# Every third row of the first expert matrix, numbers 20 to 59, on GpSimd and ScalarE in place of VectorE

## The chip, the cores and the metric

One NeuronCore of a Trainium2 chip runs the whole program. The metric is the time of one execution on the device, in microseconds (us). Engines are named as in the profile: PE (TensorE), DVE (VectorE), ACT (ScalarE), POOL (GpSimd), SP (SyncE, which issues the plain transfers). POOL also issues the gathers, which are indirect DMAs.

## The reference

The model is two transformer blocks over 256 tokens of width 2048. The change lies in the second block, in its layer of 16384 small experts (`peer`). Each of eight heads scores two sets of 128 keys, takes the best 16 of each and the best 16 of their 256 sums, which gives each token 8 x 16 = 128 expert numbers. Then, for blocks of 128 tokens:

```python
def block(args):
    xb, ib, gb = args                      # tokens, expert numbers, gates
    act = jax.nn.gelu(jnp.einsum('tkd,td->tk', expert_u[ib], xb))
    return jnp.einsum('tk,tkd->td', act * gb, expert_v[ib])
```

The first einsum is the part at hand: for each token and each of its 128 experts, the row of `expert_u` (2048 values) is multiplied by the token and summed.

## The kernel before

Most of the kernel is a long run of projections, whose weights stream in through SP. Near 1500 us in it comes to the expert layer. There are 128 tokens on the 128 partitions, so a "row" n here is one gather: for slot s = n % 128 of token block tt = n // 128, every partition fetches the row of `expert_u` that its own token asks for, 128 x 2048 values, 1 MB. There are 256 such rows, 128 for each block of tokens.

`u_rows` (L1675) is a Python generator that writes this work out. `more` (L1679) asks for gathers (`gather`, L1661, issued by POOL at L1663) while a seat is free: ten seats for the first 128 rows, four after that (`seat`, L1676; two seats share one of the five tiles `rows`). Row n + 10 takes the seat of row n. A gather also needs the expert numbers of its head: 16 slots a head. At L1703 one DVE instruction multiplies the row by the tokens (`accT`, in PSUM, called `yt` in the profile) and sums over the 2048 columns, into one column of `wv` (`sm` in the profile).

The generators of several lanes are stepped in turn, each to its next `yield`, and every engine executes its instructions in the order in which they were written out. Other lanes at this place: `topk` (L1588) finds the 16 best of each head, on DVE (L1574 to L1585, L1608 to L1613, L1619, L1620) with two small steps on POOL (L1601 and L1603, L1615); heads 5, 6 and 7 are the last. `project1` (L449) runs the query projection on PE beside it; per group j of 128 query columns ACT copies the result out of PSUM (L1546), PE makes the scores (L1555) and ACT copies those (L1557). Groups 2h and 2h + 1 belong to head h. There are three PSUM banks for projections and one for scores.

After row 127 the tokens of the second block are turned into `accT` (L1659), ACT makes the weights (L1668), and the rest of the layer follows from them: rows 128 to 255, the scatter of weights (`spots`), the second expert matrix (L1847 and L1903), then the last projections.

Of the kernel before, what the change touches and what calls it, by code (L numbers as in the profile page):

```python
# [6 lines left out]
F32 = mybir.dt.float32  # L7
# [4 lines left out]
AF = mybir.ActivationFunctionType  # L12
OP = mybir.AluOpType
# [6 lines left out]
CH = 1024  # L20
# [205 lines left out]
def program(tc, A, out, stage=99, dbg=None):  # L226
# [7 lines left out]
    hip = pool("hip", 3)  # L234
# [3 lines left out]
    def psum(name, bufs):  # L238

        p = contextlib.ExitStack()  # L240
        t = p.enter_context(tc.tile_pool(name=name, bufs=bufs, space=bass.MemoryType.PSUM))
        banks_.append(p)
        return t

    def psum_close(n):
        for _ in range(n):
            banks_.pop().close()
# [5 lines left out]
    V, S, G, PE, SP = nc.vector, nc.scalar, nc.gpsimd, nc.tensor, nc.sync  # L253
# [1264 lines left out]
    accT = rowp.tile([128, 2048], F32, name="yt", tag="yt")  # L1518
# [20 lines left out]
    wv = sm.rearrange("p a b -> p (a b)").rearrange("p (t s) -> p t s", t=2)  # L1539
# [116 lines left out]
    def turn(tt):  # L1656

        for j in range(16):
            PE.transpose(accT[:, j * 128:j * 128 + 128], xg[:, j, tt * 128:tt * 128 + 128], ident)  # L1659

    def gather(dst, src, n):  # L1661
        tt, s = divmod(n, 128)
        G.indirect_dma_start(dst, None, src, bass.IndirectOffsetOnAxis(ap=idx[:, tt, s:s + 1], axis=0))  # L1663

    def weights(tt):

        w = wv[:, tt]
        S.activation(w, w, AF.Gelu_apprx_tanh, scale=rtok[:, tt, 0:1])  # L1668
        G.tensor_mul(w, w, gate_[:, tt])
        p = pair("wt") if tt else bank(bgN, "pn")  # L1670
        PE.transpose(p[:, :128], w, ident)
        S.copy(wT[:, tt * 128:tt * 128 + 128], p[:, :128])
        flags[("w", tt)] = True

    def u_rows():  # L1675
        seat = [n % 10 if n < 128 else n % 4 for n in range(256)]  # L1676
        done, busy, ask = [0], {}, [0]

        def more(most):  # L1679

            while most and ask[0] < 256 and seat[ask[0]] not in busy and flags.get(("idx", ask[0] % 128 // 16)):
                m = ask[0]
                gather(row[seat[m]], A["w_u"], m)
                busy[seat[m]] = m
                ask[0] += 1
                most -= 1

        heads = lambda: sum(bool(flags.get(("idx", h))) for h in range(8))
        turn(0)
        while heads() < 2:  # L1690
            more(1)
            yield
        for n in range(256):
            tt, s = divmod(n, 128)
            for _ in range(2 if heads() < 8 else 0):
                more(1)
                yield
            more(2)
            while n >= ask[0]:
                yield  # L1700
                more(1)
            r = row[seat[n]]
            V.scalar_tensor_tensor(r, r, 1.0, accT, op0=OP.mult, op1=OP.mult, accum_out=wv[:, tt, s:s + 1])  # L1703
            del busy[seat[n]]
            if s == 127:
                if tt:
                    psum_close(2)
                    pairs_.update(sacc=psum("sacc", 1), tok=psum("tok", 1), wt=psum("gap", 2))
                    pairs_["sp"] = pairs_["wt"]
                else:  # L1710
                    turn(1)
                weights(tt)
            yield
        flags["u"] = True
# [144 lines left out]
    for n, lane in enumerate((2, 3, 5, 6)):  # L1859
        lanes.add(lane, topk(n, cU if n > 1 else cT))  # L1860
    lanes.add(0, slots_())
    lanes.add(4, u_rows())
    lanes.add(1, spots(0))
    lanes.add(1, spots(1))
# [100 lines left out]
```

## Time and profile before

| | |
|---|---|
| median of 3 runs | 2922.49 us (2918.72 to 2924.63) |
| the profiled execution's own time | 2921.0 us |
| its span | 2919.1 us |
| PE busy | 2292.5 us, 79% |
| DVE busy | 2002.7 us, 69% |
| ACT busy | 1185.9 us, 41% |
| POOL busy | 874.4 us, 30% |
| L1703 on DVE, 256 rows | 580.0 us |
| L1663 on POOL, 256 gathers of the first matrix | 241.6 us |

The span runs from the first to the last instruction of the profiled execution; 1.9 us of its own time lie around it. Shares of busy time are means over the whole kernel. The rows of the first matrix occupy DVE from 1554.5 to 2250.4 us. In the rows below, a bracket at the end of a timeline row tells how long the engine had been idle and what ended that.

### The profile page before, as it was taken

How to read it: one execution, taken by the hardware profiler on the slowest of the kernel's cores; microseconds unless marked ns; L12 is line 12 of the kernel's file. 1: busy time of each engine (PE TensorE's matmuls, PEld its weight loads, DVE VectorE, ACT ScalarE, POOL GpSimd, SP SyncE). 2: the span in 40 equal slices, each digit the busy share in tenths (PEclk: the TensorE clock that was granted, in tenths of full speed). 3: DMA queues.
4: the chain of work that ended last, by engine and by line, in shares of the span. 5: the costliest groups of instructions: out<-in, count | busy, mean ns of one | idle time of the engine just before them, and what ended most of it. 6: DMA issues, size and time to landing. Idle time of an engine off the chain costs nothing.

```text
span 2919.1 us, 39399 instructions
## 1 busy us (share of the span) xinstructions
PE 2292.5 (79%) x14635; PEld 2095.4 (72%) x14635; DVE 2002.7 (69%) x2641; ACT 1185.9 (41%) x2529; POOL 874.4 (30%) x1168
## 2 busy tenths in 40 slices
PE   8999999999999999999999100012211999999999
PEld 8887899888888999998998000012211988888789
DVE  5455566555556565666638999989898866666665
ACT  4355555444444454444431000058881355400043
POOL 3201215211111010223024344333333655555520
PEclk9999999999999999999999555555665699999999
DMA  6443455656655555553559889999998699999955
GB/s 224 148 130 123 125 161 179 195 188 188 194 186 192 186 174 190 171 169 109 162 186 379 347 310 422 421 400 420 401 420 346 234 397 409 409 407 409 409 200 167
DMA packets 174672, 765.09 MB, mean 262 GB/s; under 512 B 19584, under 2 KB 22048, under 8 KB 141200
## 3 DMA queue, kind: packets, MB, share of 16 engines
q1 hardware_dynamic: 99216, 353.83, 36.3%
q0 software_dynamic: 75264, 408.75, 35.0%
q8 instruction: 115, 1.88, 0.3%
q14 instruction: 77, 0.63, 0.1%
HBM read 757.77 MB, written 4.21 MB: 261 GB/s over the span
## 4 chain that ended last, share of the span: by engine, by line
PE 61%; DMA 11%; issue 10%; DVE 8%; POOL 8%; ACT 1%; POOLq 0%; SPq 0%; DVEq 0%; ACTq 0%
PE acc L411 11%; PE acc L1903 8%; PE acc L386 6%; PE acc L388 6%; PE acc L387 6%; POOL rows L1663 6%; PE acc L412 6%; DMA rows<-w_vs,idx 5%; DMA rows<-w_u,idx 4%; PE acc L485 3%; PE acc L483 3%; PE acc L484 3%; DVE rows L1703 3%; PE sp L1794 1%; DMA raw<-w_vd 1%
## 5 line engine op out<-in xcount | busy, mean ns | idle before, releaser
L350 DVE TENSOR_TENSOR wlo<-raw,whi 128x1024 fp32r<-128x1024 f32 (+1 forms) x501 | 615.2, 1236 | 390.9 <-ACT whi L349 384.0
L349 ACT CAST whi<-raw 128x1024 fp32r<-128x1024 f32 (+1 forms) x501 | 520.0, 1042 | 363.6 <-PE acc L387 131.8
L1703 DVE SCALAR_TENSOR_TENSOR rows<-rows,yt 128x2048 f32<-128x2048 f32 x256 | 580.0, 2284 | 40.8 <-DMA rows<-w_u,idx 36.6
L1903 PE MATMUL acc<-G,raw 128*128 128x256 f32 x2048 | 452.5, 382 | 11.9 <-DMA raw<-w_vd 10.9
L1903 PEld LDWEIGHTS acc<-G,raw 128*128 128x128 f32 x2048 | 388.1, 191 | 69.9 <-DMA raw<-w_vd 16.8
L1847 DVE SCALAR_TENSOR_TENSOR sacc<-rows,sm,sacc 128x1024 f32<-128x1024 f32 x254 | 327.3, 1289 | 143.4 <-DMA rows<-w_vs,idx 140.7
L1663 POOL DMA_INDIRECT rows<-w_u,idx x256 | 241.6, 944 | 392.5 <-DVE rows L1703 299.7
L1663 POOL DMA_INDIRECT rows<-w_vs,idx x256 | 247.5, 967 | 151.2 <-DVE sacc L1847 87.1
L411 PE MATMUL acc<-xl,whi 128*128 128x512 f32 x704 | 248.2, 391 | 0.0
L411 PE MATMUL acc<-xh,whi 128*128 128x512 f32 x704 | 248.1, 391 | 0.0
L1762 PE MATMUL sp<-P,Q 128*128 128x128 f32 x256 | 58.1, 419 | 213.9 <-ACT P L1758 213.9
L1762 PEld LDWEIGHTS sp<-P,Q 128*128 128x128 f32 x256 | 55.1, 327 | 217.1 <-ACT P L1758 217.1
L564 POOL TENSOR_TENSOR acc_sq<-acc_sq,sq 128x256 f32<-128x256 f32 x63 | 56.8, 902 | 500.4 <-ACT sq L563 498.8
L485 PE MATMUL acc<-ring,wlo 128*128 128x256 f32 x704 | 199.3, 283 | 0.1
L483 PE MATMUL acc<-ring,whi 128*128 128x256 f32 x704 | 199.3, 283 | 0.1
L484 PE MATMUL acc<-ring,whi 128*128 128x256 f32 x704 | 199.2, 283 | 0.0
L412 PE MATMUL acc<-xh,wlo 128*128 128x256 f32 x704 | 197.2, 280 | 0.6 <-DVE wlo L350 0.6
L412 PE MATMUL acc<-xl,wlo 128*128 128x256 f32 x704 | 197.1, 280 | 0.0
L1191 POOL TENSOR_TENSOR hT<-cF 128x256 f32<-128x256 f32 x44 | 71.8, 1632 | 372.9 <-ACT whi L349 342.9
L1659 PE MATMUL yt<-keep,xg 128*128 128x128 f32 x32 | 5.6, 350 | 201.9 <-DVE rows L1703 201.4
L386 PE MATMUL acc<-xh,whi 128*128 128x256 f32 x520 | 150.5, 289 | 3.1 <-ACT whi L349 1.8
L411 PEld LDWEIGHTS acc<-xh,whi 128*128 128x128 f32 x704 | 131.7, 187 | 28.9
(505 smaller groups left out, 5524.0 us busy)
## 6 DMA issues: line engine op xcount, KB each, us to landing
raw<-w_gu SPq DMA_DIRECT2D x176, 512.0 KB, 3.9
raw<-w_vd SPq DMA_DIRECT2D x128, 512.0 KB, 6.8
raw<-w_down SPq DMA_DIRECT2D x88, 512.0 KB, 4.4
raw<-w_out SPq DMA_DIRECT2D x32, 512.0 KB, 3.5
raw<-w_pq SPq DMA_DIRECT2D x32, 512.0 KB, 7.1
raw<-w_pg SPq DMA_DIRECT2D x32, 512.0 KB, 3.8
raw<-w_b SPq DMA_DIRECT2D x24, 512.0 KB, 3.6
raw<-w_lat SPq DMA_DIRECT2D x18, 512.0 KB, 3.7
```

The lines of the kernel that those rows point to most:

```text
L349: S.copy(hi[j][:, a:b], raw[j][:, a:b])
L350: V.tensor_sub(lo[j][:, a:b], raw[j][:, a:b], hi[j][:, a:b].bitcast(F32))
L386: PE.matmul(ps, wh, xh, start=start, stop=False, **k)
L411: PE.matmul(ps, wh, xh.both(k), start=k == 0, stop=False, skip_group_check=True)
L412: PE.matmul(ps[:, :T], wl, xh[:, k], start=False, stop=k == kb - 1, skip_group_check=True)
L483: PE.matmul(o, wh, ah, start=(k == 0 and j % 2 == 0), stop=False, skip_group_check=True)
L484: PE.matmul(o, wh, al, start=False, stop=False, skip_group_check=True)
L485: PE.matmul(o, wl, ah, start=False, stop=(k == nk - 1), skip_group_check=True)
L1663: G.indirect_dma_start(dst, None, src, bass.IndirectOffsetOnAxis(ap=idx[:, tt, s:s + 1], axis=0))
L1703: V.scalar_tensor_tensor(r, r, 1.0, accT, op0=OP.mult, op1=OP.mult, accum_out=wv[:, tt, s:s + 1])
L1847: V.scalar_tensor_tensor(sacc, r, w, sacc, op0=OP.mult, op1=OP.add)
L1903: PE.matmul(o, w, gs_[k // 16][:, k % 16], start=(k == 0 and j % 2 == 0), stop=k == 127, skip_group_check=True)
```

## The change

Of the rows 18 to 59 every third one (n % 3 == 2: rows 20, 23, ... 59, fourteen of them) is no longer done by L1703. POOL multiplies it in two halves of 1024 columns by a copy of the tokens in SBUF, in place, and ACT sums the product with an Identity activation. ACT makes the copy of the tokens once, at row 12, in two tiles of the pool `hip`. The seat of such a row is given free one row later (`late`), so that the gather which takes it stands behind the next row. In the changed kernel the lines from 1703 on have other numbers: the copies are L1710, the product L1714, the sum L1715, and the DVE instruction that was L1703 is L1718.

```diff
@@ u_rows @@
         turn(0)
+        late, yt = [], []
...
             r = row[seat[n]]
-            V.scalar_tensor_tensor(r, r, 1.0, accT, op0=OP.mult, op1=OP.mult, accum_out=wv[:, tt, s:s + 1])
-            del busy[seat[n]]
+            while late:
+                del busy[late.pop()]
+            if n == 12:
+
+                for k in range(2):
+                    yt.append(hip.tile([128, CH], F32, name="yt2", tag="whi"))
+                    S.copy(yt[k], accT[:, k * CH:k * CH + CH])
+            if 18 <= n < 60 and n % 3 == 2:
+                for k in range(2):
+                    b = r[:, k * CH:k * CH + CH]
+                    G.tensor_mul(b, b, yt[k])
+                S.activation(r, r, AF.Identity, accum_out=wv[:, tt, s:s + 1])
+                late.append(seat[n])
+            else:
+                V.scalar_tensor_tensor(r, r, 1.0, accT, op0=OP.mult, op1=OP.mult, accum_out=wv[:, tt, s:s + 1])
+                del busy[seat[n]]
```

What stands in a row on POOL, around row 20, before: the first L1663 is the gather of row 29, the two after it those of rows 30 and 31, then come the small steps of head 5's top 16. The bracket names the engines and queues whose counts an instruction waits for (DMASW are the gathers' own queues).

```order
L1663 DMA rows_15111<-w_u,idx 128x2048 [waits DMASW0_49,DVE_49]
L1663 DMA rows_15107<-w_u,idx 128x2048 [waits DMASW1_49,DVE_49]
L1663 DMA rows_15107<-w_u,idx 128x2048 [waits DMASW2_49,DVE_49]
L1601 TENSOR_TENSOR cT<-cT 128x256 x2
L1603 CAST cT<-cT 128x64 [waits DVE_49]
L1663 DMA rows_15108<-w_u,idx 128x2048 [waits DMASW3_49,DVE_49]
```

And the same place on POOL now, from behind the gather of row 29 to that of row 33:

```order
L1714 TENSOR_TENSOR rows_15107<-rows_15107,yt_15623 128x1024 [waits Activation_49]
L1714 TENSOR_TENSOR rows_15107<-rows_15107,yt_15625 128x1024 [waits Activation_49]
L1663 DMA rows_15107<-w_u,idx 128x2048 [waits DMASW1_49,Activation_49]
L1601 TENSOR_TENSOR cT<-cT 128x256 [waits DVE_49] x2
L1603 CAST cT<-cT 128x64 [waits DVE_49]
L1663 DMA rows_15107<-w_u,idx 128x2048 [waits DMASW2_49]
L1663 DMA rows_15108<-w_u,idx 128x2048 [waits DMASW3_49,DVE_49]
L1714 TENSOR_TENSOR rows_15108<-rows_15108,yt_15623 128x1024
L1714 TENSOR_TENSOR rows_15108<-rows_15108,yt_15625 128x1024
L1615 TENSOR_TENSOR cT<-cT 128x256 [waits DVE_49,Pool_49]
L1615 TENSOR_TENSOR cT<-cT 128x256 x3
L1663 DMA rows_15108<-w_u,idx 128x2048 [waits DMASW4_49,Activation_49]
```

The two products of row 20 stand behind the gather of row 29, and the gather of row 30, which is to fill row 20's seat, stands right behind the products and waits for ACT, that is for row 20's sum. The same holds for the other thirteen rows and the gathers ten rows later; behind the products of rows 23, 29 and 35 the four L1615 of heads 5, 6 and 7 come first.

On ACT, before, around the copy of query group 11 out of PSUM (the first L1546 here) and the scores of groups 11 and 12:

```order
L1546 COPY cK<-acc 128x256 [waits PE_49,Activation_49]
L1557 ACTIVATE sc<-pa,rtok 128x128 [waits PE_49]
L1557 ACTIVATE sc<-pa,rtok 128x128
L1546 COPY cK<-acc 128x256 [waits PE_49,Activation_49]
L1557 ACTIVATE sc<-pa,rtok 128x128 [waits PE_49]
```

And now:

```order
L1546 COPY cK<-acc 128x256 [waits PE_49,Activation_49]
L1715 ACTIVATE rows_15107,sm<-rows_15107 128x2048 [waits DMASW7_49,Pool_49]
L1557 ACTIVATE sc<-pa,rtok 128x128 [waits PE_49]
L1557 ACTIVATE sc<-pa,rtok 128x128
L1546 COPY cK<-acc 128x256 [waits PE_49,Activation_49]
L1715 ACTIVATE rows_15108,sm<-rows_15108 128x2048 [waits DMASW1_49,DMASW2_49,DMASW0_49,Pool_49]
L1557 ACTIVATE sc<-pa,rtok 128x128 [waits PE_49]
```

The sums of rows 20, 23, 26, 29 and 32 stand ahead of the score copies of groups 11, 12, 13, 14 and 15. On DVE nothing else moves: fourteen instructions are gone from its row.

## Rows read from the trace of the kernel before

**Rows 1.** The chain that ended last, by line, shares of the span.

```profile
PE acc L411 11%; PE acc L1903 8%; PE acc L386 6%; PE acc L388 6%; PE acc L387 6%; POOL rows L1663 6%; PE acc L412 6%; DMA rows<-w_vs,idx 5%; DMA rows<-w_u,idx 4%; PE acc L485 3%; PE acc L483 3%; PE acc L484 3%; DVE rows L1703 3%; PE sp L1794 1%; DMA raw<-w_vd 1%
```

**Rows 2.** Busy time of each engine in three stretches; clock, DMA share, GB/s.

```profile
1650.00:1700.00 50.00, 0.00 (x0) 0.00 (x0) 48.26 (x129) 0.00 (x0) 19.42 (x27) 0.50 0.68 251
1700.00:1750.00 50.00, 1.42 (x4) 0.73 (x4) 49.08 (x60) 2.57 (x6) 23.09 (x31) 0.50 0.86 335
1750.00:1800.00 50.00, 0.00 (x0) 0.00 (x0) 50.00 (x45) 0.00 (x0) 21.58 (x23) 0.50 1.01 422
```

**Rows 3.** Timeline of POOL: start, duration, line, [idle before, releaser].

```profile
1636.05 0.94 POOL L1663 DMA_INDIRECT rows<-w_u,idx  x1 [1.26 <-DVE rows L1703]
...
1670.17 1.19 POOL L1601 TENSOR_TENSOR cU<-cU 128x256 f32<-128x256 f32 x2 [2.13 <-DVE cU L1582]
1671.58 0.24 POOL L1603 CAST cU<-cU 128x64 f32<-128x64 uint32 x1 [0.22 <-DVE cU L1585]
...
1681.54 2.78 POOL L1615 TENSOR_TENSOR cU<-cU 128x256 f32<-128x256 f32 x4 [2.18 <-DVE cU L1613]
...
1734.42 0.94 POOL L1663 DMA_INDIRECT rows<-w_u,idx  x1 [1.26 <-DVE rows L1703]
1736.63 0.94 POOL L1663 DMA_INDIRECT rows<-w_u,idx  x1 [1.26 <-DVE rows L1703]
...
1813.40 0.94 POOL L1663 DMA_INDIRECT rows<-w_u,idx  x1 [0.30 <-issue]
```

**Rows 4.** L1703 counted from its start to 1846.2 and to 1922 us.

```profile
L1703 DVE SCALAR_TENSOR_TENSOR rows<-rows,yt x97: 2227/2281/2289, 1554.5 to 1843.8; 128x2048 f32<-128x2048 f32 x97
L1703 DVE SCALAR_TENSOR_TENSOR rows<-rows,yt x128: 2227/2282/2289, 1554.5 to 1921.3; 128x2048 f32<-128x2048 f32 x128
```

**Rows 5.** Timeline of DVE, rows 97 and 127.

```profile
1846.24 2.29 DVE L1703 SCALAR_TENSOR_TENSOR rows<-rows,yt 128x2048 f32<-128x2048 f32 x1 [0.19 <-DMA rows<-w_u,idx]
...
1921.34 2.29 DVE L1703 SCALAR_TENSOR_TENSOR rows<-rows,yt 128x2048 f32<-128x2048 f32 x1 [0.19 <-DMA rows<-w_u,idx]
```

**Rows 6.** L1663: its gathers up to 1636.5 us; landing of those of 1650 to 1720.

```profile
L1663 POOL DMA_INDIRECT rows<-w_u,idx x30: 939/945/1068, 1540.5 to 1636.1; - x30
DMA to landing us min/median/max: 5.3/5.6/8.5
```

**Rows 7.** Products on POOL by shape: count, busy us, mean ns.

```profile
L1191 POOL TENSOR_TENSOR hT<-cF 128x256 f32<-128x256 f32 x44 | 71.8, 1632 | 372.9 <-ACT whi L349 342.9 <-DVE cF L1190 29.9
L1789 POOL TENSOR_TENSOR P<-P,acc_sq 128x512 f32<-128x512 f32 x16 | 17.3, 1084 | 15.8 <-DVE P L1781 14.8 <-ACT acc_sq L1672 0.9
L733 POOL TENSOR_TENSOR cL<-cL 128x512 f32<-128x512 f32 x2 | 2.6, 1294 | 23.4 <-ACT cL L732 23.4
L1037 POOL TENSOR_TENSOR cC<-cC,cM 128x1024 f32<-128x1024 f32 x1 | 2.8, 2825 | 3.0 <-DMA cC<-sguw 3.0
```

**Rows 8.** ACT by shape: a pass over 1024 columns; reading out a sum.

```profile
L349 ACT CAST whi<-raw 128x1024 fp32r<-128x1024 f32 x493 | 514.0, 1047 | 359.8 <-PE acc L387 128.0 <-PE acc L484 126.4 <-PE acc L411 61.7
L928 ACT ACTIVATION_READ_ACCUMULATOR nsat<-nsat 128x1 f32 x32 | 6.0, 186 | 0.0
```

**Rows 9.** Timeline of ACT: query group 11 copied out, and its scores.

```profile
1584.07 0.37 ACT L1546 COPY cK<-acc 128x256 f32<-128x256 f32 x1 [2.88 <-PE acc L456]
1587.92 0.62 ACT L1557 ACTIVATE sc<-pa,rtok 128x128 f32<-128x128 f32 x2 [3.47 <-PE pa L1555]
```

**Rows 10.** Timeline of DVE: head 5's first steps, row 21, its next steps, row 22.

```profile
1637.91 0.87 DVE L1574 MAX8 cT<-sc 128x8 f32<-128x128 f32 x4
...
1641.55 2.27 DVE L1703 SCALAR_TENSOR_TENSOR rows<-rows,yt 128x2048 f32<-128x2048 f32 x1
1643.75 0.09 DVE L1703 DVE_READ_ACCUMULATOR rows<-rows,yt 128x1 f32 x1
...
1645.73 1.00 DVE L1574 MAX8 cT<-cT 128x8 f32<-128x256 f32 x2 [0.83 <-POOL cT L1601]
1646.64 2.27 DVE L1703 SCALAR_TENSOR_TENSOR rows<-rows,yt 128x2048 f32<-128x2048 f32 x1
```

## The prediction

> **What bounds the kernel now.** The chain of waits comes first [rows 1]: it passes through the gathers (POOL L1663, the DMA of the first matrix) and through L1703, so this stage is on the path to the end. The table of stretches comes next [rows 2]. From 1650 to 1750 us VectorE is busy 48 to 49 of 50 us and the DMA engines only 0.68 and 0.86 of theirs; from 1750 the DMA share is 1.01. So VectorE, which finds the top 16 and multiplies rows, is the limit up to about 1750, and the DMA engines after it. The timelines say the same. After the top 16, gathers leave POOL every 2.21 us and each has waited 1.26 us for L1703 to free a seat [rows 3]. From row 97 to row 127, which the counts identify [rows 4], VectorE has waited for the DMA at both ends, and 30 rows take 1921.34 - 1846.24 = 75.1 us, 2.50 us a row [rows 5]. What the first half costs is therefore read at one place: the time at which row 127 starts, 1921.34. All later work (weights, scatter, second matrix) hangs on that row and moves with it.
>
> **What the change removes.** Fourteen instructions of VectorE. At the spacing of 2.21 us [rows 3] that is 30.9 us of VectorE's time. It can bring at most what the DMA engines have idle: 0.32 x 50 + 0.14 x 50 = 23 us [rows 2].
>
> **What it adds on GpSimd.** This engine's queue is also the one that issues the gathers. I add up what stands in it from the gather of row 29 to the gather of row 69, which waits for the last sum, that of row 59. The gather of row 29 is the thirtieth and starts at 1636.05 [rows 3, 6].
> Gathers: 40 x (0.94 + 0.30 us of issue) [rows 3] = 49.6 us.
> Products: 28 of 128x1024. The trace has one such shape, 2.83 us, and 512 columns at 1.08 and 1.29 us [rows 7]; the top-16 products of 256 columns take 0.60 and 0.70 us each beside the row instructions [rows 3]. From 0.70 at 256 and 1.08 at 512 a line gives 1.86 at 1024; twice 1.08 is 2.17. I take 2.2, near the row of 1.08, and keep 1.86 and 2.83: 28 x 2.2 = 61.6 us (52 to 79).
> [...]
> Waits for sums: each of fourteen gathers stands behind a pair of products and waits until ScalarE has summed that row. A pass over 1024 columns takes 1.047 us there and reading the sum out 0.19 [rows 8]; two passes less one start-up, with the read-out, come to about 2.15, and two handovers add some 0.35: 2.5 us. In three of the fourteen places the four L1615 of a head (2.78 us [rows 3]) stand between and cover it: 11 x 2.5 = 27.5 us (bounds 1.9 and 3 us each: 21 to 33).
> Top-16 steps of heads 5, 6 and 7: 1.19 + 0.24 + 2.78 = 4.2 us each [rows 3], 12.6 us.
>
> **What it adds by ScalarE's order.** The scores of group 11, copied at 1587.92 now [rows 9], stand behind the sum of row 20, whose row is multiplied only after the gather of row 29. So they wait from about 1588 to 1644: product from 1637.0 to 1641.4, sum to 1643.6, copies to 1644.3. PE has one bank for scores, stops at those of group 12 and loses its clock (the clock is 0.50 where PE idles [rows 2]); that is hidden, because groups 13 to 15 are gated by the sums of rows 26, 29 and 32 anyway, some 10 us apart. But VectorE needs groups 10 and 11 for head 5. Its first steps take 1641.55 - 1637.91 = 3.64 us [rows 10], so they end at 1648.0 and not at 1641.55. GpSimd, done with the gather of row 30 at 1645.1, waits 2.9 us for them; then for the next steps, which stand behind row 21 (2.2 + 1.15 us, to 1651.4), 2.0 us; then for row 22 (0.9 + 2.2 us) some 1.5 us more, with the durations of [rows 10]. That is 6.4 us at head 5; heads 6 and 7 meet the same order behind rows 26 and 32: 3 x 6.4 = 19.2 us (10 to 30).
> The two copies of the tokens (2 x 1.05 us [rows 8]) fall into ScalarE's idle time, 2.9 us and more before each step there [rows 9]: nothing.
>
> **The sum.** 49.6 + 61.6 + 27.5 + 12.6 + 19.2 = 170.5 us: the gather of row 69 starts at 1806.6. By then the gathers issued before it have landed, so it lands after 5.6 us, the median where the DMA engines had idle time [rows 6], at 1812.2. From there the DMA engines are the limit as before: 58 rows x 2.50 = 145 us, and row 127 starts at 1957.2 against 1921.34, 36 us later. VectorE's 30.9 us are inside this: it waits for rows in place of multiplying them. The profiled execution took 2921.0 us, 1.9 of them outside the span, and 2921 + 36 = 2957; the median of the runs shown is 1.5 us above it. I predict 2958.
> In other words, once the top 16 is over three rows cost GpSimd 3 x 1.24 + 2 x 2.2 + 2.5 = 10.6 us, 3.5 a row, where VectorE alone took 2.21 and the DMA engines need 2.50.
>
> **The rivals.**
> First, faster: GpSimd hides its part. It is idle more than half of every stretch now (19.4 to 23.1 of 50 us busy [rows 2]), which speaks for it. If a product takes 1.9 us and the next gathers don't have to wait for the sum, three rows cost 3.72 + 3.8 = 7.5 us, just the DMA's 3 x 2.50; then VectorE's gift fills the idle DMA time and 23 us go: 2898. Against it stands the changed order: the gather behind each pair waits for ScalarE. With that wait the product would have to take 0.64 us, less than what 256 columns take.
> Second, no change: the products run at 0.7 us, so that the 170.5 us shrink by 28 x 1.5 = 42 to 128; the gather of row 69 then starts at 1764 and lands at 1770, and it need not land before 1921.34 - 145 = 1776 for row 127 to come when it does now: 2921 to 2926. Only a product of 1024 columns that costs as much as one of 256 would do it.
> Third, far slower: GpSimd and VectorE disturb each other. L1191 takes 1.63 us for 256 columns, beside conversions on VectorE, where the top-16 products take 0.60 to 0.70 [rows 3, 7]. At four times 1.63 a product costs 6.5 us, 28 x 4.3 = 120 us more: 3078. The undisturbed figures come from this very stage, with L1703 running beside them, which speaks against it. The Trainium skill (GPSIMD Engine Reference, section 1) has GpSimd share its SBUF interface with VectorE, with contention where VectorE's instruction reads two SBUF inputs or runs in a two-port mode; L1703 reads one input from PSUM, so by this rule too the time would stay at the forecast, and the chance of this rival stays small.
> That the instructions don't move as told isn't a rival: the changed order shows it.
>
> **How the numbers follow.** The forecast, GpSimd's queue as the bound of rows 20 to 69, has 0.84. Its own range: products 52 to 79 in place of 61.6, waits 21 to 33, head delays 10 to 30, not all at one end together, give -16 to +25 around 2957, so 2941 to 2982. Faster gets 0.05, no change 0.02, far slower 0.05; 0.04 is left for a smaller loss of 6 to 20 us, if heads and sums hide more than I think. The range 2938 to 2984 holds about 0.85 of this. 0.2%, 6 us, is about what a measurement of this kernel can tell from no change: faster 0.05, same 0.03, slower 0.92.
>
> **What would show it.** Right: products (L1714) of about 2.2 us; GpSimd's gathers every third time idle for 2.5 us behind ACT's L1715; after the top 16 three gathers per 10.6 us; VectorE waiting for rows between 1740 and 1810, where it waits for none now; a DMA share well under 1 up to about 1810; the scores of group 11 near 1644; row 127 near 1957; later stages of unchanged length. Wrong: products under 1 us or gathers that don't wait for L1715 (then the first two rivals), products over 4 us (the third), or a stage after row 127 that shrinks.

## The result, and the profile after

| | before | after |
|---|---|---|
| median of the runs | 2923.37 us (4 runs, 2918.72 to 2924.63) | 2968.11 us (4 runs, 2964.86 to 2972.16) |
| ratio after / before, 95% interval | | 1.0143 [1.0122, 1.0163] |
| profiled execution / its span | 2921.0 / 2919.1 us | 2972.16 / 2970.4 us |
| start of row 0 (first row instruction on VectorE) | 1554.52 us | 1563.21 us |
| start of row 127 | 1921.34 us | 1972.03 us |
| row 0 to row 127 | 366.8 us | 408.8 us |
| row 127 to the end of the span | 997.8 us | 998.4 us |

The change makes the kernel slower: by 44.7 us between the medians (1.53%), by 1.43%, some 42 us, in the ratio. 2958 was forecast, and the forecast range holds the result. Of the 50.7 us by which row 127 starts later in the two profiles, 8.7 are there before row 0, ahead of all that the change touches: the 1408 matmuls of the projection at L411 took 399 ns each in this execution and 391 ns in the other, 9 us in all; why they did stays open. The stage between row 0 and row 127 is longer by 42.0 us, and all that follows has kept its length.

The stretches of the changed kernel, to be held against [rows 2] (columns: window, length, busy us of PE, PEld, DVE, ACT and POOL with their instructions, granted clock, DMA share, GB/s):

```profile
1650.00:1700.00 50.00, 26.30 (x92) 21.36 (x92) 38.46 (x117) 8.90 (x16) 30.71 (x27) 0.70 0.68 255
1700.00:1750.00 50.00, 2.14 (x7) 1.47 (x7) 40.30 (x80) 9.46 (x16) 34.00 (x35) 0.50 0.54 195
1750.00:1800.00 50.00, 0.50 (x2) 0.18 (x1) 24.06 (x23) 10.45 (x12) 35.81 (x24) 0.50 0.83 308
1800.00:1850.00 50.00, 0.00 (x0) 0.00 (x0) 38.38 (x34) 4.00 (x4) 31.14 (x27) 0.50 0.89 348
```

VectorE is no longer the limit: of 50 us it is busy 24 between 1750 and 1800, where it was busy 50. But the DMA engines have not taken over. Their share sinks to 0.54 between 1700 and 1750 (0.86 before) and stays below 1.01 up to 1850. Neither of the two engines of [rows 2] is full, so a third sets the pace, and it is not one with a high busy share either: POOL stands at 31 to 36 of 50.

POOL's timeline shows what it does. First the steady cycle after the top 16, to be held against [rows 3]; the columns are start, duration, engine, line, and in brackets the idle time before it with what ended it:

```profile
1761.60 4.67 POOL L1714 TENSOR_TENSOR rows<-rows,yt 128x1024 f32<-128x1024 f32 x2
1768.57 0.98 POOL L1663 DMA_INDIRECT rows<-w_u,idx  x1 [2.31 <-ACT rows L1715]
1769.86 0.95 POOL L1663 DMA_INDIRECT rows<-w_u,idx  x1 [0.30 <-DVE rows L1718]
1771.11 0.95 POOL L1663 DMA_INDIRECT rows<-w_u,idx  x1 [0.30 <-issue]
1772.08 2.35 POOL L1714 TENSOR_TENSOR rows<-rows,yt 128x1024 f32<-128x1024 f32 x1
```

From one pair of products to the next it takes 1772.08 - 1761.60 = 10.48 us, three gathers of which the first stands idle 2.31 us for ScalarE's sum: 3.5 us a row, where the DMA engines need 2.50. The forecast for this cycle was 10.6 us.

Then the place around row 20 in the same view, where the sum blocks the scores:

```profile
1646.82 0.94 POOL L1663 DMA_INDIRECT rows<-w_u,idx  x1 [1.26 <-DVE cT L1574]
1647.78 4.64 POOL L1714 TENSOR_TENSOR rows<-rows,yt 128x1024 f32<-128x1024 f32 x2
1654.73 0.98 POOL L1663 DMA_INDIRECT rows<-w_u,idx  x1 [2.31 <-ACT sc L1557]
1657.98 1.20 POOL L1601 TENSOR_TENSOR cT<-cT 128x256 f32<-128x256 f32 x2 [2.27 <-DVE cT L1582]
1661.60 0.24 POOL L1603 CAST cT<-cT 128x64 f32<-128x64 uint32 x1 [2.42 <-DVE cT L1585]
1661.99 0.98 POOL L1663 DMA_INDIRECT rows<-w_u,idx  x1
1664.65 0.95 POOL L1663 DMA_INDIRECT rows<-w_u,idx  x1 [1.69 <-DVE rows L1718]
```

and ScalarE's timeline of the same time:

```profile
1578.05 0.37 ACT L1546 COPY cK<-acc 128x256 f32<-128x256 f32 x1 [2.88 <-PE acc L456]
1614.38 1.93 ACT L1710 COPY yt<-yt 128x1024 f32<-128x1024 f32 x2 [35.96 <-DVE rows L1718]
...
1652.46 1.91 ACT L1715 ACTIVATE rows<-rows 128x2048 f32<-128x2048 f32 x1 [29.28 <-POOL rows L1714]
1654.27 0.19 ACT L1715 ACTIVATION_READ_ACCUMULATOR rows<-rows 128x1 f32 x1
1654.36 0.61 ACT L1557 ACTIVATE sc<-pa,rtok 128x128 f32<-128x128 f32 x2
```

The scores of group 11 (L1557, the last line) are copied from 1654.36 to 1654.97. On the clock of before (8.7 us less) that ends at 1646.3, where 1644.3 was forecast. A releaser has to be read with care here: POOL's gather at 1654.73 names "ACT sc L1557", but its seat is that of row 20, so it waited for the sum at 1652.46, whose release ScalarE gave about the time at which it began the scores. On VectorE's timeline, row 12 stops for the copies of the tokens, and later the first step of head 5 for these scores:

```profile
1616.34 2.29 DVE L1718 SCALAR_TENSOR_TENSOR rows<-rows,yt 128x2048 f32<-128x2048 f32 x1 [1.99 <-ACT yt L1710]
...
1654.74 0.68 DVE L1574 MAX8 cT<-sc 128x8 f32<-128x128 f32 x3 [7.98 <-ACT sc L1557]
```

The first line is one that the prediction did not have: the copies at row 12 (L1710, above) wait 35.96 us for VectorE to have read the tokens' tile in row 11, and VectorE's row 12 waits 1.99 us for the copies. Both engines only read that tile in PSUM, and yet in this trace they take turns at it. The second line has its like at heads 6 and 7; the three waits come to 21.8 us of VectorE's time (13.8 in the line below and the 7.98 above):

```profile
DVE cU L1574 <- ACT sc L1557: 13.8, 2, 8.0
```

The durations by shape, L1714 being the product, L1715 the sum and L1718 the row instruction on VectorE (min, median and max in ns, first and last start):

```profile
L1714 POOL TENSOR_TENSOR rows<-rows,yt x28: 2340/2356/2372, 1647.8 to 1816.2; 128x1024 f32<-128x1024 f32 x28
...
L1718 DVE SCALAR_TENSOR_TENSOR rows<-rows,yt x242: 2228/2287/2290, 1563.2 to 2299.4; 128x2048 f32<-128x2048 f32 x121
...
L1715 ACT ACTIVATE rows<-rows x14: 1909/1909/1911, 1652.5 to 1818.6; 128x2048 f32<-128x2048 f32 x14
L1715 ACT ACTIVATION_READ_ACCUMULATOR rows<-rows x14: 185/186/188, 1654.3 to 1820.4; 128x1 f32 x14
```

No sign is seen of one engine slowing the other: all 28 products lie within 32 ns, those of 1700 to 1750, where VectorE is busy 40 of 50 us, as well as those of 1750 to 1800, where it is busy 24, and VectorE's rows have kept 2.28 us [rows 4]. The rival with contention is out by this view alone, and so is the one with a cheap product.

### The profile page after: what moved, and what is told of

It is laid out like the page before. It is cut to its first block, busy times and chain, and to the rows that moved or that the text cites. A ratio compares the mean times of both kernels' runs of the same rounds, so it can differ in the third digit from the quotient of the medians.

```text
span 2970.4 us, 39454 instructions
## 1 busy us (share of the span) xinstructions
PE 2311.7 (78%) x14635; PEld 2100.0 (71%) x14635; DVE 1981.8 (67%) x2613; ACT 1215.9 (41%) x2559; POOL 941.5 (32%) x1196
## 4 chain that ended last, share of the span: by engine, by line
PE 60%; DMA 11%; issue 10%; POOL 9%; DVE 8%; ACT 1%; SPq 0%; POOLq 0%; ACTq 0%; DVEq 0%
PE acc L411 11%; PE acc L1918 8%; PE acc L386 6%; PE acc L388 6%; PE acc L387 6%; DMA rows<-w_u,idx 6%; PE acc L412 5%; POOL rows L1663 5%; DMA rows<-w_vs,idx 5%; PE acc L485 3%; PE acc L483 3%; PE acc L484 3%; DVE rows L1718 2%; PE sp L1809 1%; POOL rows L1714 1%
## 5 line engine op out<-in xcount | busy, mean ns | idle before, releaser
L1718 DVE SCALAR_TENSOR_TENSOR rows<-rows,yt 128x2048 f32<-128x2048 f32 x242 | 552.0, 2285 | 82.9 <-DMA rows<-w_u,idx 76.5
L1663 POOL DMA_INDIRECT rows<-w_u,idx x256 | 242.3, 947 | 369.9 <-DVE rows L1718 229.3
L1663 POOL DMA_INDIRECT rows<-w_vs,idx x256 | 248.2, 969 | 145.0 <-DVE sacc L1862 68.4
L411 PE MATMUL acc<-xl,whi 128*128 128x512 f32 x704 | 252.7, 399 | 0.0
L411 PE MATMUL acc<-xh,whi 128*128 128x512 f32 x704 | 252.7, 399 | 0.0
L411 PEld LDWEIGHTS acc<-xh,whi 128*128 128x128 f32 x704 | 132.3, 188 | 32.9
```

The source lines that it names most:

```text
L411: PE.matmul(ps, wh, xh.both(k), start=k == 0, stop=False, skip_group_check=True)
```

## The experiments

All are built on the changed kernel. Since the time before row 0 differs from run to run, each was read in two ways: by its ratio to the kernel before, and by the stage from row 0 to row 127 in its profile (366.8 us before, 408.8 after). A stage is read from one profiled execution; the only kernel of the experiments that was profiled twice gave 359.2 and 360.2 us, so a difference of 1 to 2 us says little.

**Seats given back one product later.** The gather behind a pair of products then takes the seat of the row before that.

```
-            while late:
-                del busy[late.pop()]
+            while len(late) > (n < 60):
+                del busy[late.pop(0)]
```

> The seat of a row that GpSimd multiplied is given back one such row later, so that the gather behind a pair of products takes a seat whose sum is long done; products, sums and ScalarE's order stay. Theory A (GpSimd's queue: products and waits for sums between its gathers): after the top 16 three rows cost 10.46 - 2.31 = 8.15 us, the waits <-ACT L1715 of POOL go (17.3 + 6.9 us, about 24), row 127 comes some 20 to 25 us earlier than with the change, +20 to +25 us against the kernel before. Theory B (what costs is ScalarE's order: the score copies that stand behind sums make the top 16 late): the scores stay blocked, so the loss stays, +40 to +45. Theory C (it is the products alone): +40 too, since the waits only move to another place.

Measured: 2956.02 us, ratio 1.0085 [1.0062, 1.0108], +25 us; row 0 to row 127 takes 391.5 us, 17.3 less than with the change. POOL's timeline no longer has the wait:

```profile
1746.87 4.66 POOL L1714 TENSOR_TENSOR rows<-rows,yt 128x1024 f32<-128x1024 f32 x2
1751.69 0.99 POOL L1663 DMA_INDIRECT rows<-w_u,idx  x1 [0.16 <-issue]
1752.98 0.94 POOL L1663 DMA_INDIRECT rows<-w_u,idx  x1 [0.30 <-issue]
1754.23 0.95 POOL L1663 DMA_INDIRECT rows<-w_u,idx  x1 [0.30 <-issue]
1755.20 4.64 POOL L1714 TENSOR_TENSOR rows<-rows,yt 128x1024 f32<-128x1024 f32 x2
```

Three rows take 8.33 us, and yet the scores of group 11 still come at 1652.48. So the gathers' waits for the sums are a cost of their own, of about 17 us; theories B and C, which left the loss at 40, are out as explanations of the whole. The rest, +25, is still there.

**Products without sums.**

```
-                S.activation(r, r, AF.Identity, accum_out=wv[:, tt, s:s + 1])
```

> The fourteen sums on ScalarE are left out (so these rows have no result); the products on GpSimd stay. This takes away both the gathers' waits for sums and what blocks the score copies. Theory A: of the 170.5 us reckoned in GpSimd's queue, the 27.5 of waits and the 19.2 of head delays go, the products' 65 stay: row 127 comes 35 to 45 us earlier than with the change, 0 to +10 us against the kernel before; three rows after the top 16 take 8.1 to 8.4 us. Theory C (the products alone bound it): +30 or more, as with the change. Theory D (VectorE's relief of 30.9 us is real once the waits are gone): -15 to -20, faster than before.

Measured: 2934.46 us, ratio 1.0017 [0.9995, 1.0038]; 374.6 us from row 0 to row 127, 16.9 less than with the seats alone held back. The three rows take 8.4 us as in the run before, so what has gone in addition is the blocking of the scores. The products alone are not what bounds it, and VectorE's relief does not outweigh them either.

**Sums without products.**

```
-                for k in range(2):
-                    b = r[:, k * CH:k * CH + CH]
-                    G.tensor_mul(b, b, yt[k])
```

> The 28 products on GpSimd are left out: ScalarE sums fourteen rows that were not multiplied (so their results are wrong in value), and VectorE is still relieved of fourteen instructions. Theory A: 65 us leave GpSimd's queue, and a sum can start when its row lands; the gathers are then set by VectorE's rows and the DMA engines, and VectorE's relief can fill the DMA time that stood idle before, at most 23 us: -8 to -20 us against the kernel before. Theory B (ScalarE's order is what costs): the sums still stand before the score copies, so +15 or more stays. Theory C (relief of VectorE is worth nothing): 0.

Measured: 2914.77 us, ratio 0.9960 [0.9941, 0.9979], -12 us; 356.2 us from row 0 to row 127, 10.6 less than before the change. Fourteen rows fewer on VectorE are thus worth something; between this run and the one with products and no sums lie 374.6 - 356.2 = 18.4 us. It also shows about what handing over these rows could bring if the products cost nothing: 11 us, or 13 without the stop of 2.0 us for the copies, which is still there; the prediction's upper bound was the 23 us of idle DMA time.

The windows of this run show why (same columns as above):

```profile
1650.00:1700.00 50.00, 1.22 (x4) 0.93 (x4) 47.35 (x139) 6.85 (x11) 23.89 (x32) 0.50 0.78 306
1700.00:1750.00 50.00, 1.42 (x4) 0.73 (x4) 39.28 (x37) 16.86 (x21) 25.00 (x32) 0.50 1.00 403
```

From 1700 the DMA engines are full and VectorE idles; up to 1700 they are at 0.78 and VectorE is still the limit, with the top 16 in hand. In this run only relief that comes before 1700 can count, and rows 38 to 59 come after it: VectorE starts row 39 at 1701.84.

**The copies at row 0.** The line `if n == 12:` becomes `if n == 0:`.

> Only the two copies of the tokens are moved, from row 12 to row 0, where ScalarE is not behind a row of VectorE that has yet to land. Theory A with the copies as a term of their own: VectorE's stop of 1.99 us at row 12 goes and the kernel is 2 us faster than with the change. Theory A as predicted (copies cost nothing): no difference. A rival: at row 0 the copies stand before copies that PE waits for, and cost 2 to 4 us there as well.

Measured: 2967.38 us, ratio 1.0139 [1.0098, 1.0181], which can't be told from the change's 1.0143. The stage from row 0 to row 127 is 406.6 us, 2.2 less, and the stop of 1.99 us at row 12 is gone from VectorE. The copies now run at 1543.31, before row 0, when VectorE does not yet read the tile. A term of 2 us is below what the times can decide; the trace of one execution agrees with it.

**The same instructions, the sum issued three rows later.**

```
-            while late:
-                del busy[late.pop()]
+            while late and (n >= late[0][0] + 3 or n >= 63):
+                m, b = late.pop(0)
+                S.activation(b, b, AF.Identity, accum_out=wv[:, 0, m:m + 1])
+                del busy[seat[m]]
...
-                S.activation(r, r, AF.Identity, accum_out=wv[:, tt, s:s + 1])
-                late.append(seat[n])
+                late.append((n, r))
```

> All fourteen rows, their 28 products, their sums and the copies stay as in the change; only the place of the sum in ScalarE's order moves: the sum of a row is issued three rows later, just ahead of the next products, and the seat is given back then. So ScalarE does not stand at a sum whose products are still to come, and the scores' copies pass. Theory A (two waits make most of the loss: GpSimd's gathers for the sums, and the scores' copies behind them): both go, and what stays is the products' 65 us in GpSimd's queue against VectorE's relief, as where the sums were left out: +3 to +10 us against the kernel before, three rows in 8.3 to 8.4 us after the top 16, scores of group 11 before 1630. Rival (the sums' own time on ScalarE, or their reads of SBUF beside the others, cost what leaving them out gave back): +25 or more. Rival (a seat kept three rows longer starves the gathers): +15 to +30.

Measured: 2936.09 us, ratio 1.0040 [1.0022, 1.0057], +12 us; 377.2 us from row 0 to row 127, 2.6 more than without any sum. ScalarE's timeline shows the scores of group 11 at 1620.86, ahead of the first sum, which still stops the groups after them:

```profile
1620.86 0.62 ACT L1557 ACTIVATE sc<-pa,rtok 128x128 f32<-128x128 f32 x2 [3.47 <-PE acc L456]
1624.37 0.37 ACT L1546 COPY cK<-acc 128x256 f32<-128x256 f32 x1 [2.88 <-PE acc L456]
1646.16 1.91 ACT L1706 ACTIVATE rows<-rows 128x2048 f32<-128x2048 f32 x1 [21.42 <-POOL rows L1716]
```

VectorE has no wait for scores left in its list of waits. Three quarters of the loss (31.6 of 42.0 us in the stage) were not the work that was added but its place in two queues: the same 28 products and 14 sums, issued in another order, cost 10 us in place of 42. Held against the run with seats given back later (391.5 us), which also keeps the seats longer and differs in where the sums stand, this run puts the price of the blocked scores at 14.3 us.

**Only rows 20 to 35, and only rows 38 to 59.** The condition becomes `18 <= n < 36` in the one and `36 <= n < 60` in the other.

> Only the six rows 20 to 35 go to GpSimd, as in the change; rows 38 to 59 are VectorE's again. Theory A: blocked scores, the head delays and five or six waits for sums stay, 28 us of products are added to a stretch in which VectorE's relief (6 x 2.21 = 13 us) is of use: +12 to +20 us against the kernel before. Rival (the loss is made after the top 16, where GpSimd takes 10.46 us for three rows and the DMA engines 7.5): 0 to +5. Rival (the loss is all in the blocked scores of groups 11 to 15): +40.

> Only the eight rows 38 to 59 go to GpSimd, as in the change; rows 20 to 35 are VectorE's, so no score copy waits behind a sum. Theory A: three rows take 10.46 us of GpSimd's queue where the kernel before takes 6.63 and the DMA engines 7.5, so eight times 2.96 to 3.83: +24 to +31 us against the kernel before. Rival (blocked scores are the cost): 0 to +5. Rival (VectorE's relief of 8 x 2.21 = 18 us is of use here too): +5 to +13. If theory A holds here and for rows 20 to 35 alone, the two losses add up to about the whole one.

Measured: 2945.98 us, ratio 1.0068 [1.0047, 1.0090], +20 us for the early six; 2954.64 us, 1.0102 [1.0081, 1.0123], +30 us for the late eight, where 24 to 31 were expected. The stage from row 0 to row 127 grows by 17.0 and 27.1 us, together 44.1, against 42.0 for all fourteen (the copies' 2 us are in both). So the loss is made in both places and by different means: the late rows, with no score behind them, pay the cycle of 10.5 us eight times and get nothing for VectorE's relief; the early ones pay for scores and sums. For the early six the upper end of the expectation was met and not passed; either rival (0 to 5, or all of 40) is out.

**A version from these readings.** Five rows, 15 to 31 in steps of four, the sums three rows later, the copies at row 0:

```
+            while late and (n >= late[0][0] + 3 or n >= 38):
...
+            if n == 0:
...
+            if 14 <= n < 34 and n % 4 == 3:
```

> What the runs so far point to: only five rows, 15 to 31 in steps of four, in the stretch where VectorE was the limit and the DMA engines stood partly idle; each sum issued three rows later on ScalarE, so that neither gathers nor scores wait for it; the copies at row 0. Theory A: 5 x 2.21 = 11 us of VectorE's work go from the stretch that VectorE limits, the products (5 x 4.67 = 23 us) stand in GpSimd's idle time, and row 127 comes 3 to 9 us earlier than in the kernel before: 2914 to 2921 against 2923. Rival (GpSimd's queue delays gathers even here, or the later top 16 steps): 0 to +10 us. Rival (relief of VectorE brings nothing as long as GpSimd multiplies): 0.

Measured: 2921.79 us, ratio 0.9989 [0.9972, 1.0006]: not to be told from no change. In its profile row 127 starts 359.2 us after row 0, 7.6 less than before, but the rows from 128 on took 324.6 us, 3.8 more. It was timed again, beside a version with six rows (20 to 35 in steps of three):

> The version with five rows, 15 to 31 in steps of four, timed again, since its first interval, 0.9972 to 1.0006, holds both a gain and none. Theory A: the 7.6 us that row 127 comes earlier stay in the end, ratio 0.997 to 0.999. Rival: the second half of the rows gives them back (324.6 us from row 128 to row 255 in its first profile, 320.8 in the kernel before), ratio 1.000.

> The same with six rows, 20 to 35 in steps of three (the rows of the first six in the change), sums three rows later, copies at row 0. Theory A: 6 x 2.21 = 13 us leave VectorE in the stretch that it limits, 28 us of products stand in GpSimd's queue, closer together than in the version with five rows: -3 to -8 us against the kernel before, where the same six rows with their sums issued at once cost +20. Rival (three rows of 8.3 us on GpSimd are too slow even before the top 16 has ended): 0 to +8.

Measured, on another chip: five rows 2916.60 us, ratio 0.9957 [0.9944, 0.9970]; six rows 2921.98 us, 0.9979 [0.9962, 0.9996]. In the second profile of the five rows, the stage up to row 127 is 360.2 us, and the rows from 128 on took 321.7. Its windows, to be held against [rows 2]:

```profile
1650.00:1700.00 50.00, 8.43 (x24) 6.61 (x24) 48.14 (x133) 8.19 (x14) 31.30 (x32) 0.57 0.77 304
1700.00:1750.00 50.00, 1.42 (x4) 0.73 (x4) 49.18 (x47) 1.28 (x5) 25.07 (x32) 0.50 0.99 402
```

The DMA share is 0.77 and 0.99 where it was 0.68 and 0.86, with VectorE as full as before: the rows that GpSimd took made room, and the room was filled. The gain shows in one timing of two; in the other its interval holds no gain as well. Where it shows, it is larger than was expected (0.997 to 0.999): 0.9957 is 12.6 us, and the stage of its profile explains 6.6 of them. With six rows the ratio stands for 6 us, and the stage, 365.1 us in its profile, for 1.7. So how much these versions bring is not settled. What made the rows from 128 on vary between 318.8 and 326.7 us over the profiles of these runs, with nothing changed in that stage, stays open.

## Why the prediction was right, step by step

**The bound.** It named GpSimd's in-order queue from the gather of row 29 to that of row 69 as what would set the end, and took 170.5 us for it. The trace has 1820.88 - 1646.82 = 174.06 us. Its terms, from the groups and waits of POOL in that stretch, the wait of the gather of row 69 included:

| term | forecast | measured |
|---|---|---|
| 28 products | 61.6 us (2.2 each) | 65.2 us (2.33 each; the two of a pair overlap a little) |
| gathers waiting for sums | 27.5 us (11 x 2.5) | 24.2 us (eleven waits: 17.3 named L1715, 6.9 named L1557) |
| top-16 steps of three heads | 12.6 us | 12.7 us (8.4 of L1615, 3.6 of L1601, 0.7 of L1603) |
| 40 gathers | 49.6 us | 49.6 us, taken as forecast |
| delays of the heads and the rest | 19.2 us | 22.4 us, what is left of 174.06 |

The row that carries the products, and the waits that stand for the sum (total, number, longest):

```profile
L1714 POOL TENSOR_TENSOR rows<-rows,yt 128x1024 f32<-128x1024 f32 x28 | 65.2, 2355 | 0.2
POOL rows L1663 <- ACT rows L1715: 17.3, 8, 2.3
POOL rows L1663 <- ACT sc L1557: 6.9, 3, 2.3
```

**The gathers' wait for the sum** was 2.30 or 2.31 us in ten of the eleven places, and not 2.5; at the eleventh it was 1.14, since other work of POOL covered half. The pass over 2048 columns with its read-out took 2.00 us (1.91 and 0.19, overlapping by 0.1) where 2.15 had been put together from passes over 1024, and what is left, the two handovers, 0.31 us where 0.35 had been put without a row to show it. That the wait is on the path is shown by the run with held seats. There the gather of row 69 starts 152.1 us after that of row 29, 21.9 us sooner than with the change, so that nearly all of the 24.2 us came back in this stretch. From that gather to row 127 it then takes 155.8 us in place of 151.2, as the DMA engines are the limit there (from 1806.8 on POOL's gathers wait some 1.5 us each for the DMA). What is left is the 17.3 us of the stage.

**ScalarE's order** was foreseen with its mechanism. At head 5 POOL waits 2.27 + 2.42 + 1.69 = 6.4 us in the timeline above; 2.9 + 2.0 + 1.5 = 6.4 were forecast. The prediction gave heads 6 and 7 the same 6.4 us each; the waits at the same place take 3.4 us at head 6 and 5.9 us at head 7, 15.7 in all for the 19.2 of the term. What the order costs in the end is 16.9 us (seats held against no sums) or 14.3 (seats held against sums issued later), inside the range of 10 to 30.

**From the gather of row 69 to row 127** 5.6 + 145 = 150.6 us were forecast; the trace has 1972.03 - 1820.88 = 151.15. Everything behind row 127 was to keep its length, and did (998.4 against 997.8 us).

**What was mis-sized.** The copies of the tokens were priced at nothing, as work in ScalarE's idle time. The price was not ScalarE's time but VectorE's: 1.99 us of wait at row 12, as the two engines take turns at the tile in PSUM. It is seen at the start of the stretch too: from row 0 to the gather of row 29 it took 83.6 us, 81.5 before. The copies also held up ScalarE's queue: the scores of group 9 come at 1616.19, 34 us later than before on the same clock. No cost of that is seen, as VectorE's list of waits has none for these scores. The products were 0.13 us longer each, 3.6 us in all. With the two the forecast of +36 becomes +42, the 42.0 of the stage. That it comes out so near is partly luck: the waits for sums were 3.3 us shorter and the last term of the table 3.2 us longer, and the two cancel. The other 2 to 3 us of the 44.7 in the medians are within what executions of this kernel differ by.

**The rivals.** The faster one (GpSimd hides its part) asked for products of 1.9 us and gathers that do not wait; with sums out of the way three rows still took 8.4 us, not 7.5, and the loss did not become a gain. No change asked for products of 0.7 us, far slower for 6.5 us; 2.33 settles both. The Trainium skill (GPSIMD Engine Reference, section 3.1) has 4497 ns for an addition of two tensors over 2048 columns on GpSimd. Half of it, 2.25 us, is an estimate for 1024 columns; the products here took 2.34 to 2.37, some 5% more. By the Trainium skill (GPSIMD Engine Reference, section 1) GpSimd and VectorE contend where VectorE's instruction has two SBUF inputs or runs in a two-port mode. The trace agrees as far as it goes: the row instructions, with one input in PSUM, kept 2.28 us while products ran beside them; the other case was not examined.

**The ledger of the 42 us**, from one run to the next in the stage from row 0 to row 127: VectorE's relief, with sums and copies in place, -10.6; the products +18.4; the blocked scores +16.9; the gathers' waits for sums +17.3. Taken away in another order the four would share out somewhat differently: both products and sums in place, with only the order mended, stood at +10.4, and not at -10.6 + 18.4 = +7.8. The step to the products also takes the sums away, and the step to the blocked scores brings them back and holds the seats longer, so each figure is that of a step and not of one cause alone.

## What to carry to other kernels

An engine with half of its time idle isn't free if its queue also issues the transfers that the stage lives on: count what will stand between two issues, waits included, and hold it against the time that one transfer needs. When work is handed from engine to engine, the place of the last piece in its queue matters as much as its length: issued three rows later, where less that the stage needs stands behind them, the same sums and products cost 10 us here, and 42 where gathers and scores waited behind them. And relief is worth something only in the stretch that the relieved engine limits: find it by the windows, and leave rows outside of it alone.

## What the runs showed of the hardware that was not expected

- GpSimd's product of 128x1024 f32 in SBUF took 2.34 to 2.37 us in all 28 cases, whether VectorE was busy 40 or 24 of 50 us; the one row of that shape in the kernel before [rows 7], 2.83 us, was no guide.
- ScalarE's pass over 2048 columns took 1.909 us, 1.82 times the 1.047 us for 1024 [rows 8]; the read-out of the sum 0.186 us.
- A gather that waited for the products of its own engine stood 0.27 us behind them (the run without sums), one that waited for ScalarE's sum 2.31, of which 0.31 are neither the pass nor the read-out, which take 2.00 together.
